# A weighted sum of pairs of rows: from four buffers of 12 tokens to three rooms of 16, combined token by token

## The chip, the cores and the metric

The kernel runs on one core of a Trainium2 chip. The metric is the device time of one execution in microseconds (us); the median of three runs is compared before and after. The profile is one execution recorded by the hardware profiler. Engines that matter here: VectorE (DVE) and ScalarE (ACT) do arithmetic on data in on-chip memory, which has 128 partitions; SyncE (SP) and ACT issue transfers (DMA) between main memory and on-chip memory. Each of the two issuing engines has one transfer queue (q1 for SP, q10 for ACT), and both queues run on the same 16 DMA engines.

## The reference

```python
batch, seq, hidden, n_experts, k = 16, 1024, 512, 8, 2
expert_outputs : float32 [batch, seq, k, hidden]
combine_weights: float32 [batch, seq, k]

def reference(expert_outputs, combine_weights):
    weights = combine_weights[..., np.newaxis]
    return np.sum(expert_outputs * weights, axis=2).astype(np.float32)
```

There are 16 x 1024 = 16384 tokens. For each, two rows of 512 floats (4 KB together) are read, each is multiplied by its own weight, and their sum (2 KB) is written: 67.1 MB in, 33.6 MB out, and 0.13 MB of weights.

## The kernel before

Every partition handles 128 tokens (`per`). The first 120 of them (`main`) come from one contiguous stretch of main memory per partition, so the rows of neighbouring partitions lie 120 x 4 KB = 480 KB apart in the input and 240 KB apart in the output. The last 8 (`LAST`) come from a second region, the end of the arrays, with 32 KB and 16 KB between partitions. `rows` (lines 34 to 38) builds these two views.

The tokens are cut into ten tiles of 12 and one of 8 (`J`, `LAST`, loop at line 68). A tile `et` is one of four buffers of a pool (line 50), 48 KB per partition. Loads are issued by SP (line 75). The first tile is loaded in two pieces, 2 tokens and 10 tokens, and the 2-token piece is cut into rows of 4 KB (line 78); all other loads move one row per partition: 40 KB, 48 KB, and 32 KB for the last tile. A load into a buffer that was used before waits until the store of that buffer has landed.

There are three ways to combine. Tiles 0 to 8 take two long VectorE instructions each: line 84 multiplies the whole tile by the weights, broadcast along the row, and line 85 adds the two halves and writes the sums packed into the front of the same buffer (`ot`). Their store is issued by ACT (line 86). Tile 9 has its first halves scaled by ACT, one token per instruction (line 92), its second halves by one VectorE instruction (line 107), and the sum by another (line 108). Tile 10, the last, is worked token by token: ACT scales the first half (line 92), and VectorE multiplies the second half by its weight and adds (line 96). The stores of tiles 9 and 10 are issued by SP (line 109).

Ahead of the loop, VectorE zeroes a small tile `zt` (line 56), and ACT issues, in this order: a store of `zt` to 16 spots of the output that are overwritten later (line 58), the load of the weights of the main tokens, 960 B per partition, the load of the weights of the last 8 tokens, 64 B per partition (line 62), and a one-column activation that brings in the activation table (line 66). `tc.issue_after` keeps this order.

Waits between engines are made by the framework from the regions that instructions read and write, and the order of instructions on each engine is the framework's own.

Of the kernel before, what the change touches and what calls it, by code (L numbers as in the profile page):

```python
# [1 line left out]

# [4 lines left out]


@with_exitstack
def kernel(  # L10
    ctx: ExitStack,
    tc: tile.TileContext,
    expert_outputs: bass.AP,
    combine_weights: bass.AP,
    out: bass.AP,
):

    nc = tc.nc  # L20
    b, s, k, h = expert_outputs.shape
    assert k == 2
    n = b * s
    P = nc.NUM_PARTITIONS
    per = n // P
    assert per * P == n
    J, LAST = 12, 8
    main = per - LAST
    assert main % J == 0
    eo = expert_outputs.rearrange("b s k h -> (b s) (k h)")  # L30
    cw = combine_weights.rearrange("b s k -> (b s) k")
    o = out.rearrange("b s h -> (b s) h")

    def rows(x):

        a = x[0 : P * main, :].rearrange("(p t) f -> p t f", p=P)
        b = x[P * main : n, :].rearrange("(p t) f -> p t f", p=P)
        return lambda t, c: a[:, t : t + c, :] if t < main else b[:, t - main : t - main + c, :]

    eo, cw, o = rows(eo), rows(cw), rows(o)  # L40

    dt = mybir.dt.float32
    mult = mybir.AluOpType.mult
    add = mybir.AluOpType.add
    copy = mybir.ActivationFunctionType.Copy

    last = main // J

    wpool = ctx.enter_context(tc.tile_pool(name="w", bufs=1))
    ipool = ctx.enter_context(tc.tile_pool(name="in", bufs=4))  # L50

    wt = wpool.tile([P, per * k], dt)


    zt = wpool.tile([16, 128], dt)
    nc.vector.memset(zt, 0.0)  # L56
    first = out.rearrange("b s h -> (b s) h")[0 : P * main, :].rearrange("(q t) h -> q (t h)", q=16)
    ahead = nc.scalar.dma_start(out=first[:, 0:128], in_=zt)  # L58

    with tc.issue_after(ahead.ins):  # L60
        for t, c in ((0, main), (main, LAST)):
            nc.scalar.dma_start(
                out=wt[:, k * t : k * (t + c)].rearrange("p (t k) -> p t k", k=k), in_=cw(t, c)
            )
        warm = wpool.tile([P, 1], dt)
        nc.scalar.activation(out=warm, in_=nc.const_aps.tensor(1.0, (P, 1), dt), func=copy)  # L66

    for g in range(last + 1):
        et = ipool.tile([P, J, k * h], dt)

        ot = et.rearrange("p j f -> p (j f)")[:, 0 : J * h].rearrange("p (j f) -> p j f", f=h)
        t0, c = g * J, J if g < last else LAST

        for a, m in ((0, 2), (2, c - 2)) if g == 0 else ((0, c),):
            nc.sync.dma_start(  # L75
                out=et[:, a : a + m],
                in_=eo(t0 + a, m),
                max_dma_last_dim=k * h * 4 if g + a == 0 else None,
            )
        if g < last - 1:  # L80

            wb = wt[:, g * J * k : (g + 1) * J * k].unsqueeze(2).to_broadcast([P, J * k, h])
            ek = et.rearrange("p j (k h) -> p (j k) h", k=k)
            nc.vector.tensor_tensor(out=ek, in0=ek, in1=wb, op=mult)  # L84
            nc.vector.tensor_tensor(out=ot, in0=et[:, :, 0:h], in1=et[:, :, h : 2 * h], op=add)  # L85
            nc.scalar.dma_start(out=o(t0, c), in_=ot)
            continue


        for i in range(c):  # L90
            t = t0 + i
            nc.scalar.activation(  # L92
                out=et[:, i, 0:h], in_=et[:, i, 0:h], func=copy, scale=wt[:, 2 * t : 2 * t + 1]
            )
            if g == last:
                nc.vector.scalar_tensor_tensor(  # L96
                    out=ot[:, i, :],
                    in0=et[:, i, h : 2 * h],
                    scalar=wt[:, 2 * t + 1 : 2 * t + 2],
                    in1=et[:, i, 0:h],  # L100
                    op0=mult,
                    op1=add,
                )
        if g < last:
            w1 = wt.rearrange("p (t k) -> p t k", k=k)[:, t0 : t0 + c, 1:2]
            x1 = et[:, :, h : 2 * h]
            nc.vector.tensor_tensor(out=x1, in0=x1, in1=w1.to_broadcast([P, c, h]), op=mult)  # L107
            nc.vector.tensor_tensor(out=ot, in0=et[:, :, 0:h], in1=x1, op=add)  # L108
        nc.sync.dma_start(out=o(t0, c), in_=ot[:, 0:c])


# [1 line left out]
_INS = ['expert_outputs', 'combine_weights']  # L113
_OUTS = [((16, 1024, 512), 'float32')]


# [23 lines left out]
```

## Time and profile before

| quantity | value |
|---|---|
| time, median of 3 runs | 239.11 us (239.08 to 239.12) |
| span of the profiled execution | 237.3 us |
| DVE busy | 194.1 us (82%), 29 instructions |
| ACT busy | 14.0 us (6%), 22 instructions |
| main memory read / written | 67.24 MB / 33.56 MB |
| load of a 12-token tile, issue to landing (median) | 29.9 us |
| store of a 12-token tile from ACT, issue to landing (median) | 33.0 us |
| load of the main weights, issue to landing | 17.0 us |
| last load landed | 219.8 us |
| last store issued / landed | 226.5 us / 236.5 us |

The span is counted from the first instruction to the last of the profiled execution, the time also holds what lies around it. "Busy" is the time in which an engine executed instructions; a transfer's time from issue to landing includes its turns behind other transfers on the same engines.

SP, which issues all loads, mostly waits until a buffer is free again:

```profile
SPq L75 <- DMA out_dram<-et: 174.1, 7, 45.8
SPq L75 <- DMA et<-in_expert_outputs_dram: 15.0, 2, 12.2
SPq L109 <- DVE et L108: 14.1, 1, 14.1
SPq L109 <- DMA et<-in_expert_outputs_dram: 10.3, 2, 7.8
```

The columns are the waiting queue and line, what it waited for, the total in us, how often, and the longest.

### The profile page before, as it was taken

What the parts mean: (1) busy time and instruction counts of PE and PEld (TensorE: products, weight loads), DVE (VectorE), ACT (ScalarE), POOL (GpSimd) and SP (SyncE); (2) the same over time, 40 slices, a digit from 0 to 9 for tenths busy, and PEclk for the clock granted to TensorE, in tenths of its full rate; (3) what the DMA queues carried; (4) which work ended last, traced back from release to release, by engine and by line L of the source; (5) the groups of instructions that cost most, each with busy time, mean ns of one, the idle gap of its engine ahead of it and who ended that gap; (6) DMA issues with size and microseconds to landing.
All of it is one profiled execution on the core that took longest, in us unless ns stands there. A gap on an engine that the chain in (4) does not pass through costs nothing.

```text
span 237.3 us, 157 instructions
## 1 busy us (share of the span) xinstructions
DVE 194.1 (82%) x29; ACT 14.0 (6%) x22; POOL 0.2 (0%) x4
## 2 busy tenths in 40 slices
DVE  0008999999999999999999889969996998785710
ACT  2000000000000000000000000000000000740800
POOL 0000000000000000000000000000000000000000
DMA  7999999989899999999898999999998979999997
GB/s 289 452 474 398 398 448 480 398 356 505 352 443 435 427 464 464 398 398 530 348 514 348 447 418 443 464 464 398 398 522 348 522 344 451 464 398 442 406 434 309
DMA packets 3760, 100.80 MB, mean 425 GB/s; under 512 B 544, under 2 KB 688, under 8 KB 944
## 3 DMA queue, kind: packets, MB, share of 16 engines
q1 hardware_dynamic: 2144, 72.35, 71.0%
q10 hardware_dynamic: 1616, 28.45, 27.9%
HBM read 67.24 MB, written 33.56 MB: 425 GB/s over the span
## 4 chain that ended last, share of the span: by engine, by line
DMA 59%; DVE 34%; ACT 2%; ACTq 0%; DVEq 0%; issue 0%; SPq 0%
DMA out_dram<-et 29%; DMA et<-in_expert_outputs_dram 23%; DVE et L84 22%; DVE et L85 11%; DMA wt<-in_combine_weights_dram 7%; ACT et L92 2%; DVE et L96 1%; DVEq L135 0%; ACTq L135 0%; ACTq L58 0%; DVE zt L56 0%; DVEq L84 0%; SPq L75 0%; ACTq L92 0%
## 5 line engine op out<-in xcount | busy, mean ns | idle before, releaser
L84 DVE TENSOR_TENSOR et<-et,wt 128x12288 f32<-128x12288 f32 x9 | 116.6, 12955 | 24.1 <-DMA wt<-in_combine_weights_dram 17.5
L85 DVE TENSOR_TENSOR et<-et 128x6144 f32<-128x6144 f32 x9 | 59.0, 6557 | 0.3
L92 ACT ACTIVATE et<-et,wt 128x512 f32<-128x512 f32 x20 | 12.5, 708 | 208.6 <-DMA et<-in_expert_outputs_dram 208.6
L96 DVE SCALAR_TENSOR_TENSOR et<-et,wt 128x512 f32<-128x512 f32 x8 | 5.6, 746 | 3.9 <-ACT et L92 3.6
L107 DVE TENSOR_TENSOR et<-et,wt 128x6144 f32<-128x6144 f32 x1 | 6.6, 6557 | 2.3 <-DMA et<-in_expert_outputs_dram 2.3
L108 DVE TENSOR_TENSOR et<-et 128x6144 f32<-128x6144 f32 x1 | 6.6, 6558 | 0.9 <-ACT et L92 0.9
L66 ACT ACT_TABLE_LOAD x1 | 1.3, 1283 | 2.4 <-issue 2.4
L56 DVE MEMSET zt<- 16x128 f32 x1 | 0.2, 165 | 0.8 <-PEq L124 0.8
L66 ACT ACTIVATE warm<-const-float32-1.0 128x1 f32<-128x1 f32 x1 | 0.2, 202 | 0.0
L124 POOL MEMSET const-bfloat16-1.0<- 128x1 bf16 x1 | 0.1, 102 | 0.0
L124 POOL MEMSET const-uint8-127<- 128x1 uint8 x1 | 0.1, 101 | 0.0
L124 POOL MEMSET const-float32-0.0<- 128x1 f32 x1 | 0.1, 99 | 0.2 <-issue 0.2
L124 POOL MEMSET const-float32-1.0<- 128x1 f32 x1 | 0.1, 98 | 0.0
## 6 DMA issues: line engine op xcount, KB each, us to landing
et<-in_expert_outputs_dram SPq DMA_DIRECT2D x9, 6144.0 KB, 29.9
out_dram<-et ACTq DMA_DIRECT2D x9, 3072.0 KB, 33.0
et<-in_expert_outputs_dram SPq DMA_DIRECT2D x1, 5120.0 KB, 17.0
et<-in_expert_outputs_dram SPq DMA_DIRECT2D x1, 4096.0 KB, 25.1
out_dram<-et SPq DMA_DIRECT2D x1, 3072.0 KB, 14.6
out_dram<-et SPq DMA_DIRECT2D x1, 2048.0 KB, 10.0
et<-in_expert_outputs_dram SPq DMA_DIRECT2D x1, 1024.0 KB, 5.0
wt<-in_combine_weights_dram ACTq DMA_DIRECT2D x1, 120.0 KB, 17.0
```

The source lines that it names most:

```text
L56: nc.vector.memset(zt, 0.0)
L66: nc.scalar.activation(out=warm, in_=nc.const_aps.tensor(1.0, (P, 1), dt), func=copy)
L84: nc.vector.tensor_tensor(out=ek, in0=ek, in1=wb, op=mult)
L85: nc.vector.tensor_tensor(out=ot, in0=et[:, :, 0:h], in1=et[:, :, h : 2 * h], op=add)
L92: nc.scalar.activation(out=et[:, i, 0:h], in_=et[:, i, 0:h], func=copy, scale=wt[:, 2 * t : 2 * t + 1])
L96: nc.vector.scalar_tensor_tensor(out=ot[:, i, :], in0=et[:, i, h : 2 * h], scalar=wt[:, 2 * t + 1 : 2 * t + 2], in1=et[:, i, 0:h], op0=mul ...
L107: nc.vector.tensor_tensor(out=x1, in0=x1, in1=w1.to_broadcast([P, c, h]), op=mult)
L108: nc.vector.tensor_tensor(out=ot, in0=et[:, :, 0:h], in1=x1, op=add)
L124: nc = _bacc.Bacc("TRN2", target_bir_lowering=False, num_devices=1)
```

## The change

The four buffers become one tile `et` with three rooms of 16 tokens (64 KB per partition each). The tiles have 4, 12 and then seven times 16 tokens; tile g uses room g mod 3. The main part has 112 tokens per partition (448 KB between neighbouring partitions in the input, 224 KB in the output), the last tile's 16 tokens come from the second region (64 KB and 32 KB). No load is cut into smaller rows by hand any more.

All tiles are combined token by token, by `combine`: ACT scales the first half, VectorE multiplies the second half and adds. The sums are packed at the front of the room. For tile 6 alone the tokens are taken from the last to the first and the sums packed at the back of room 0, and tile 7's sums lie at the front of room 1 behind it, so that the two tiles go out in one store of 32 rows of 2 KB, 64 KB per partition. There are eight stores for nine tiles. ACT issues the first six; SP issues the pair's and the last. After a store is issued, SP's next load into that room follows in program order (`load(g + ROOMS)`).

The weights of the main tokens are loaded by SP, between load 0 and load 1; those of the last 16 tokens by ACT behind the store of `zt`. `tc.manual_schedule()` keeps the instructions of each engine in the order in which the program lists them.

```diff
-    J, LAST = 12, 8
-    main = per - LAST
+    ROOM, ROOMS = 16, 3
+    TILES = [4, 12, 16, 16, 16, 16, 16, 16, 16]
+    STORES = [[0], [1], [2], [3], [4], [5], [6, 7], [8]]
+    main = per - TILES[-1]
+    starts = [sum(TILES[:g]) for g in range(len(TILES))]
...
-    wpool = ctx.enter_context(tc.tile_pool(name="w", bufs=1))
-    ipool = ctx.enter_context(tc.tile_pool(name="in", bufs=4))
-    wt = wpool.tile([P, per * k], dt)
+    pool = ctx.enter_context(tc.tile_pool(name="all", bufs=1))
+    et = pool.tile([P, ROOMS * ROOM, k * h], dt)
+    halves = et.rearrange("p j (k h) -> p (j k) h", k=k)
+    wt = pool.tile([P, per * k], dt)
...
+    def load(g):
+        at, c = g % ROOMS * ROOM, TILES[g]
+        nc.sync.dma_start(out=et[:, at : at + c], in_=eo(starts[g], c))
+
+    def weights(q, t, c):
+        q.dma_start(out=wt[:, k * t : k * (t + c)].rearrange("p (t k) -> p t k", k=k), in_=cw(t, c))
+
+    def combine(g, up):
+        at, c = g % ROOMS * ROOM, TILES[g]
+        base = k * at + (ROOM if up else 0)
+        for i in range(c - 1, -1, -1) if up else range(c):
+            t = k * (starts[g] + i)
+            x0, x1 = halves[:, k * (at + i), :], halves[:, k * (at + i) + 1, :]
+            nc.scalar.activation(out=x0, in_=x0, func=copy, scale=wt[:, t : t + 1])
+            nc.vector.scalar_tensor_tensor(
+                out=halves[:, base + i, :], in0=x1, scalar=wt[:, t + 1 : t + 2], in1=x0, op0=mult, op1=add
+            )
+        return base
...
-        for t, c in ((0, main), (main, LAST)):
-            nc.scalar.dma_start(
-                out=wt[:, k * t : k * (t + c)].rearrange("p (t k) -> p t k", k=k), in_=cw(t, c)
-            )
...
+    with tc.manual_schedule():
+        nc.vector.memset(zt, 0.0)
+        ahead = flat[0 : P * main, :].rearrange("(q t) h -> q (t h)", q=16)
+        nc.scalar.dma_start(out=ahead[:, 0:128], in_=zt)
+        weights(nc.scalar, main, per - main)
         nc.scalar.activation(out=warm, in_=nc.const_aps.tensor(1.0, (P, 1), dt), func=copy)
...
-        for a, m in ((0, 2), (2, c - 2)) if g == 0 else ((0, c),):
-            nc.sync.dma_start(
-                out=et[:, a : a + m],
-                in_=eo(t0 + a, m),
-                max_dma_last_dim=k * h * 4 if g + a == 0 else None,
-            )
-        if g < last - 1:
-            wb = wt[:, g * J * k : (g + 1) * J * k].unsqueeze(2).to_broadcast([P, J * k, h])
-            ek = et.rearrange("p j (k h) -> p (j k) h", k=k)
-            nc.vector.tensor_tensor(out=ek, in0=ek, in1=wb, op=mult)
-            nc.vector.tensor_tensor(out=ot, in0=et[:, :, 0:h], in1=et[:, :, h : 2 * h], op=add)
-            nc.scalar.dma_start(out=o(t0, c), in_=ot)
-            continue
...
+        load(0)
+        weights(nc.sync, 0, main)
+        for g in range(1, ROOMS):
+            load(g)
+        for j, st in enumerate(STORES):
+            bases = [combine(g, up=len(st) == 2 and g == st[0]) for g in st]
+            c = sum(TILES[g] for g in st)
+            q = nc.sync if j >= len(STORES) - 2 else nc.scalar
+            q.dma_start(out=o(starts[st[0]], c), in_=halves[:, bases[0] : bases[0] + c, :])
+            for g in st:
+                if g + ROOMS < len(TILES):
+                    load(g + ROOMS)
```

More of the change, by code (lines that the diff above doesn't have):

```diff
@@ L26 @@
     assert per * P == n
-    J, LAST = 12, 8
-    main = per - LAST
[L29 to L32, printed above, removed]
-    def rows(x):
[L36 to L40, printed above, removed]
+    ROOM, ROOMS = 16, 3
+    TILES = [4, 12, 16, 16, 16, 16, 16, 16, 16]
+    STORES = [[0], [1], [2], [3], [4], [5], [6, 7], [8]]
+    assert sum(TILES) == per and [g for st in STORES for g in st] == list(range(len(TILES)))
+    main = per - TILES[-1]
+    starts = [sum(TILES[:g]) for g in range(len(TILES))]
+    def rows(x):
+        first = x[0 : P * main, :].rearrange("(p t) f -> p t f", p=P)
+        second = x[P * main : n, :].rearrange("(p t) f -> p t f", p=P)
+        return lambda t, c: first[:, t : t + c, :] if t < main else second[:, t - main : t - main + c, :]
+    flat = out.rearrange("b s h -> (b s) h")
+    eo = rows(expert_outputs.rearrange("b s k h -> (b s) (k h)"))
+    cw = rows(combine_weights.rearrange("b s k -> (b s) k"))
+    o = rows(flat)
     dt = mybir.dt.float32
@@ L45 @@
     copy = mybir.ActivationFunctionType.Copy
-    last = main // J
-    wpool = ctx.enter_context(tc.tile_pool(name="w", bufs=1))
-    ipool = ctx.enter_context(tc.tile_pool(name="in", bufs=4))
-    wt = wpool.tile([P, per * k], dt)
[L55 to L60, printed above, removed]
-        for t, c in ((0, main), (main, LAST)):
-            nc.scalar.dma_start(
-                out=wt[:, k * t : k * (t + c)].rearrange("p (t k) -> p t k", k=k), in_=cw(t, c)
-            )
-        warm = wpool.tile([P, 1], dt)
-        nc.scalar.activation(out=warm, in_=nc.const_aps.tensor(1.0, (P, 1), dt), func=copy)
@@ L68 @@
[L68 to L72, printed above, removed]
-        for a, m in ((0, 2), (2, c - 2)) if g == 0 else ((0, c),):
-            nc.sync.dma_start(
-                out=et[:, a : a + m],
-                in_=eo(t0 + a, m),
-                max_dma_last_dim=k * h * 4 if g + a == 0 else None,
-            )
-        if g < last - 1:
-            wb = wt[:, g * J * k : (g + 1) * J * k].unsqueeze(2).to_broadcast([P, J * k, h])
-            ek = et.rearrange("p j (k h) -> p (j k) h", k=k)
-            nc.vector.tensor_tensor(out=ek, in0=ek, in1=wb, op=mult)
-            nc.vector.tensor_tensor(out=ot, in0=et[:, :, 0:h], in1=et[:, :, h : 2 * h], op=add)
-            nc.scalar.dma_start(out=o(t0, c), in_=ot)
-            continue
[L90 to L93, printed above, removed]
-            )
[L95 to L109, printed above, removed]
@@ new lines @@
+    pool = ctx.enter_context(tc.tile_pool(name="all", bufs=1))
+    et = pool.tile([P, ROOMS * ROOM, k * h], dt)
+    halves = et.rearrange("p j (k h) -> p (j k) h", k=k)
+    wt = pool.tile([P, per * k], dt)
+    zt = pool.tile([16, 128], dt)
+    warm = pool.tile([P, 1], dt)
+    def load(g):
[3 more added lines that the diff above has]
+        q.dma_start(out=wt[:, k * t : k * (t + c)].rearrange("p (t k) -> p t k", k=k), in_=cw(t, c))
@@ new lines @@
+    with tc.manual_schedule():
[3 more added lines that the diff above has]
+        weights(nc.scalar, main, per - main)
+        nc.scalar.activation(out=warm, in_=nc.const_aps.tensor(1.0, (P, 1), dt), func=copy)
+        load(0)
[5 more added lines that the diff above has]
+            c = sum(TILES[g] for g in st)
+            assert bases[-1] == bases[0] + sum(TILES[g] for g in st[:-1])
+            q = nc.sync if j >= len(STORES) - 2 else nc.scalar
[3 more added lines that the diff above has]
+                    load(g + ROOMS)
```

## The prediction

> **What bounds the kernel now.** I read the transfer rows first, because the kernel does three arithmetic operations on every pair of floats that it loads.
>
> ```profile
> DMA  7999999989899999999898999999998979999997
> DMA packets 3760, 100.80 MB, mean 425 GB/s; under 512 B 544, under 2 KB 688, under 8 KB 944
> q1 hardware_dynamic: 2144, 72.35, 71.0%
> q10 hardware_dynamic: 1616, 28.45, 27.9%
> ```
>
> The two queues together fill 98.9% of sixteen engines' span. Fine windows show where the rest is:
>
> ```profile
> 2.00:3.00 1.00, 0.00 (x0) 0.62 (x1) 0.00 (x0) 1.00 0.70 172
> 20.00:40.00 20.00, 19.97 (x3) 0.00 (x0) 0.00 (x0) 1.00 1.00 433
> 40.00:60.00 20.00, 19.96 (x3) 0.00 (x0) 0.00 (x0) 1.00 0.98 413
> 235.00:236.00 1.00, 0.00 (x0) 0.00 (x0) 0.00 (x0) 1.00 0.62 262
> 236.00:237.00 1.00, 0.00 (x0) 0.00 (x0) 0.00 (x0) 1.00 0.00 0
> ```
>
> The columns are the window, its length, DVE, ACT and POOL busy time, clock, DMA share and GB/s. Transfers run without a hole from the ramp at the start to a cut-off at 236; a share over 1 in neighbouring windows only means that a packet is counted where it ends. So the end is set by how long the transfer engines need for their bytes. The arithmetic is hidden, though DVE is busy for 194 of 237 us:
>
> ```profile
> L84 DVE TENSOR_TENSOR et<-et,wt 128x12288 f32<-128x12288 f32 x9 | 116.6, 12955 | 24.1 <-DMA wt<-in_combine_weights_dram 17.5
> L85 DVE TENSOR_TENSOR et<-et 128x6144 f32<-128x6144 f32 x9 | 59.0, 6557 | 0.3
> L92 ACT ACTIVATE et<-et,wt 128x512 f32<-128x512 f32 x20 | 12.5, 708 | 208.6 <-DMA et<-in_expert_outputs_dram 208.6
> L96 DVE SCALAR_TENSOR_TENSOR et<-et,wt 128x512 f32<-128x512 f32 x8 | 5.6, 746 | 3.9 <-ACT et L92 3.6
> ```
>
> The chain of waits puts 34% on DVE, but during those stretches the transfers ran at full rate; it tells what released what, not what would save time.
>
> **An account of the 237.3 us.** The packet records give one packet's time on its engine: 4 KB 0.159 us, 16 KB 0.611, 24 KB 0.912, 32 KB 1.213, 48 KB 1.815. Every 8 KB adds 0.301 us, which is 27.2 GB/s an engine, 435.2 for sixteen; 100.80 MB take 231.6 us by that. Starts of neighbouring 4 KB packets on one engine are 0.155 us apart, where 4 KB at 27.2 GB/s are 0.1506, so a packet costs about 0.005 us besides its bytes. There are 3760/16 = 235 packets an engine (26 of them semaphore writes): 1.2 us. In the first three microseconds 0.77 us are lost (first packets of 4 KB took 0.195 to 1.07 us in place of 0.159). When the first real store joins, 16 load packets started near 41 took 1.93 to 2.33 us and 15 near 47 took 1.91 to 2.25, about 0.55 us lost in all. 231.6 + 1.2 + 0.77 + 0.55 = 234.1; the packets run from 1.79 to 236.14, which is 234.35, the last 0.2 being engines that finish apart. Ahead lie 1.79 us, behind 1.2 (landing 0.34, then the closing barrier), together the span of 237.3. The median of the runs, 239.11, is 1.8 above it; I take these 1.8 as fixed.
>
> **Part by part.** DVE loses nine pairs of 12.96 + 6.56 us, two instructions of 6.56 and eight of 0.75; it gains 128 of 0.75. ACT goes from 20 to 128 instructions of 0.71. Both are costed at nothing, with the transfers as cover. What matters is the time of one tile from landing to its last instruction. In the last tile of before, eight DVE instructions took 5.78 us and started 0.76 after ACT's first; their starts were 0.86 apart for the first three, 0.66 after. So 4 tokens take 4.0 us, 12 take 9.3, 16 take 12. If that cover were gone, 12 us would stand open at the end.
>
> *Packets.* Loads: before 16 (the 4 KB pieces) + 8 + 72 + 8 = 104 an engine; after 8 + 8 + 7 x 8 = 72. Stores: before 72 + 8 + 8 = 88, after 8 + 8 + 32 + 8 + 8 = 64. Weights (16) and the zero tile (1) stay. Semaphore packets 26 to 20. In sum 235 to 173: 62 x 0.005 = -0.31 us. The bytes stay. A 64 KB packet is not in the trace; by the line it takes 2.418. If a 64 KB row goes as two packets, 64 more an engine come back (+0.32).
>
> *Start.* The first load has 16 KB rows in place of 4 KB ones. Its cold first packets aren't shown; the loss is bounded by none (-0.77) and by the loss of before on top of itself (+0.77). I take -0.1: idle engines between small packets (13 to 15 busy between 2.1 and 2.8) cost some 0.1 and go, the first-touch latency stays.
>
> *First store.* The dip of 0.55 can stay (0) or go (-0.55). I leave it. Until 41 the kernel only loads, and 48 KB packets took 1.819 to 1.831 there; stores start at about 17 now, and that saves 0.004 a packet or so: -0.05.
>
> *Weights.* The 112 tokens' weights leave ACT's queue, where they took 17.0 us to land because each of 8 packets an engine took turns with a load packet; on SP's they follow load 0 and need 8 x 0.04. SP issues four transfers at the start, as before; load 1 is issued one slot of 0.46 us later, behind load 0's 4.9 us. Nothing. The 16 tail tokens' weights stay on ACT and are wanted at about 207.
>
> *Token-wise waits.* ACT now issues a store behind its tile's DVE work; queued behind it is only the next tile, which waits for its load anyway. Regions of one tile don't wait for each other: the two transfers into `wt` were in flight together, and DVE started on the first at 18.5 while the second landed at 33.0. So one `et` for all rooms is no wait in itself.
>
> *Three rooms.* Load g+3 waits for store g. Does a queue run dry? The queues take turns by packet, so a load and a store of 16 tokens take 8 x (2.418 + 1.213) = 29 us together. Step by step: load 0 drains at 7.2, weights at 7.6, store 0 is issued at 12, load 1 drains at 23, store 0 at 37 (its 8 KB packets wait turns behind load 2's 64 KB ones), load 3 is issued there; load 2 drains at 47, store 1 at 63, load 3 at 74, and from there everything repeats with 29: stores 2, 3, 4, 5 drain at 92, 121, 150, 180, loads 4 to 7 at 103, 132, 161, 187. Each load is issued 9 to 10 us before the one ahead has drained, and each store lies queued 5 us before the one ahead ends. Load 8 is issued at 180 with load 7 still moving until 187. Then it has the engines to itself until 206; tile 7 is combined at 199.5, so the pair's 64 KB rows are queued 7 us in time and last until 225.6; tile 8, landed at 207, is combined at 219, 6 us in time; its store drains at 235.3. No hole, the tightest cover being 5 us.
>
> The sum: -0.31 - 0.1 - 0.05 = -0.46, rounded to -0.5: span 236.8, time **238.6**.
>
> **The pitch.** Rows of the main part lie 448 KB apart (input), 480 before. In before, packets took their straight-line time at 480 KB, and at 32 KB in the tail; the slowest undisturbed read-only packet, 1.831 for 1.815, is 0.9% more. That row is the bound: 0.9% of 154 us of load bytes is +1.4 us; the other end is 0. I take 0, since 48 KB packets beside stores took 1.815 throughout.
>
> The Trainium skill, "DMA: Bandwidth & Descriptors", section "Latency and other measured facts", speaks against the change: it gives 207 GB/s a direction for rows 512 KiB apart against 214 padded, and less for larger powers of two. By 207/214 the estimate would be 8 us more; 448 KB is seven times 64 KB and no power of two; the trace has no row at either of these pitches, and at 480 KB it shows no loss.
>
> **Rivals.** (1) The saving is given back: 64 KB rows cut in two (+0.32), or the longer instruction streams of ACT and DVE (20 to 128, 29 to about 130) fetched while running; six 8 KB fetches lie ahead of the span in the trace, 0.31 to 0.57 us of an engine each. The program does need more code; against it speaks that one engine's delay only shows if it ends last. 238.6 + 0.32 to 0.6 is 238.9 to 239.2. Chance 0.12.
> (2) Slower, by the pitch: load packets over 2.418 from tile 2 on, at +1.4: 240.0. It decides from 0.6% on a load packet. Chance 0.10.
> (3) Slower, by the end: no third store is queued while tiles 6 and 7 wait for one another, so load 8 alone must hide tile 7's arithmetic. It decides once a token takes over 1.14 us ((206 - 187.5)/16). If ACT and DVE alternated (0.71 + 0.75), 16 tokens would take 23.4: a hole of 5 at 206 and one of 4 before the last store: 247.6. The 5.78 us for eight tokens speak against. Chance 0.04.
> (4) The one tile makes hidden waits, so the overlap isn't what the code says: a store's issue to landing of some 25 us laid open once would give 263. Chance 0.02.
>
> **How the numbers follow.** The fed queue holds 0.72, its own range 237.9 (start loss and half of the dip gone) to 239.1 (start worse by 0.5). A measurement of this kernel tells about 0.2%, 0.48 us, from no change: below 238.63 is faster. Of the 0.72 I give 0.42 to faster, 0.30 to the same band; rival 1 adds 0.08 to same and 0.04 to slower through a fetch on the last engine and a worse start; rivals 2 to 4 add 0.16 to slower. The range runs from 237.9 to 239.9: it holds case 1 and reaches toward rival 2's 240.0.
>
> **What would show it.** Right: 2768 packets, 100.80 MB, DMA tenths of 9 throughout, load packets of 2.42, DVE near 95 us, the weights landed by 9 us, load 8 issued before load 7 has landed. 3792 packets mean cut rows. A hole in the windows near 187 or 206 is rival 3; a lower rate with full share is rival 2. The prediction falls if the last packet ends later than 236.1 with 2768 packets.

## The result and the profile after

The changed kernel takes 240.58 us (median of 8 executions, 240.53 to 241.05) against 239.13 for the kernel before on the same chip: 1.006 times as long, with a 95% interval of 1.0048 to 1.0072. That is 1.45 us slower, where 0.5 us less was forecast. The profiled execution took 240.75.

The page of the changed kernel, its transfer rows:

```profile
DMA  7999999999999999989899999989899989899994
DMA packets 2771, 100.83 MB, mean 422 GB/s; under 512 B 448, under 2 KB 592, under 8 KB 592
q1 hardware_dynamic: 1728, 79.81, 77.9%
q10 hardware_dynamic: 1040, 21.00, 20.4%
q14 instruction: 3, 0.02, 0.0%
```

There are 2768 data and semaphore packets, as counted in the prediction, and three more on a third queue that the page of before doesn't have: instructions, fetched while the kernel runs. Transfers have no hole, and the two arithmetic engines are far from being a bound:

```profile
L74 DVE SCALAR_TENSOR_TENSOR et<-et,wt 128x512 f32<-128x512 f32 x128 | 87.2, 745 | 132.1 <-ACT et L73 130.3
L73 ACT ACTIVATE et<-et,wt 128x512 f32<-128x512 f32 x128 | 79.4, 708 | 135.6 <-DMA et<-in_expert_outputs_dram 130.3
```

The schedule is the predicted one. In the timeline, tile 7 starts at 189.1 and the pair's store is issued at 201.0, while load 8 (issued at 181.9) moves until 206.8 to 208.1:

```profile
189.12 9.91 ACT L73 ACTIVATE et<-et,wt 128x512 f32<-128x512 f32 x16 [15.32 <-DMA et<-in_expert_outputs_dram]
189.87 11.07 DVE L74 SCALAR_TENSOR_TENSOR et<-et,wt 128x512 f32<-128x512 f32 x16 [14.16 <-ACT et L73]
200.97 19.70 SPq L96 DMA_DIRECT2D out_dram<-et  x2
```

The time went where the prediction had no term. Fine windows at the end (window, length, the engines' busy time, clock, DMA share, GB/s; a packet is counted in the window in which it starts):

```profile
234.00:235.00 1.00, 0.00 (x0) 0.00 (x0) 0.00 (x0) 1.00 1.06 459
235.00:236.00 1.00, 0.00 (x0) 0.00 (x0) 0.00 (x0) 1.00 0.46 197
236.00:237.00 1.00, 0.00 (x0) 0.00 (x0) 0.00 (x0) 1.00 0.08 33
237.00:238.00 1.00, 0.00 (x0) 0.00 (x0) 0.00 (x0) 1.00 0.00 0
```

In before no packet of data starts after 236; here one still does, a store row of 32 KB that takes 1.21 us, hence the share of 0.08. When each engine wrote its semaphore for the last transfer says the same more sharply (us behind the first engine, from the trace's packet records):

```
before: first at 235.70  0 .02 .11 .14 .18 .21 .21 .24 .25 .25 .26 .27 .32 .34 .41 .43
after:  first at 235.76  0 .01 .09 .15 .17 .20 .21 .23 .23 .33 .55 1.10 1.12 1.29 1.33 1.79
```

The first engine ends where it did. Five engines end 0.7 to 1.4 us later than any did before, and the kernel waits for the last one. Bytes done against 27.2 GB/s an engine give the mean over the engines: 2.89 us behind at 235.5, where before it was 2.51. So of 1.41 us by which the last packet ends later (236.14 to 237.55), 0.38 are in the mean and 1.03 in the spread (the last engine is 1.24 behind the mean, 0.21 before).

**Two things made engines late.** The first is a stall when the first stores join. The packets are timed against the straight line of 0.301 us per 8 KB. In the changed kernel load packets of 48 KB lose 0.03 to 0.31 us at 13 to 22, when store 0 joins, and those of 64 KB lose 0.25 to 1.09 at 35 to 42, when store 1 joins; in the mean 0.32 and 0.79 us an engine. In before it is 0.56, at 41 to 49. The windows show the second one (few packets start from 35 to 40, since those that started near 37 are drawn out):

```profile
30.00:35.00 5.00, 3.85 (x6) 2.13 (x4) 0.00 (x0) 1.00 1.03 441
35.00:40.00 5.00, 0.00 (x0) 0.00 (x0) 0.00 (x0) 1.00 0.74 256
40.00:45.00 5.00, 0.00 (x0) 0.00 (x0) 0.00 (x0) 1.00 1.17 505
```

The stall of before, in its own windows:

```profile
40.00:45.00 5.00, 5.00 (x1) 0.00 (x0) 0.00 (x0) 1.00 0.98 393
45.00:50.00 5.00, 5.00 (x1) 0.00 (x0) 0.00 (x0) 1.00 0.92 378
```

It is uneven: load 2 drains on twelve engines between 47.57 and 47.81, on the other four 2.0 us later, and a tile later these four are still 1.05 to 1.23 behind. The second thing is the fetches. VectorE has 208 instructions on record, ACT 152 (48 and 52 before, with their semaphore waits). Fetches of 8 KB take 0.309 us on one engine at 83.7 (VectorE is then at its 70th instruction), 93.2 (ACT at its 62nd) and 217.4 (VectorE at its 200th). The load packet beside each is lengthened by 0.533, 0.241 and 0.458. With the fetch itself that is 0.84, 0.55 and 0.77 us, and the list of offsets changes by those amounts: from load 3 to load 4 one engine moves from 0.18 to 1.02 and one from 0 to 0.55, and from load 8 to the pair's store one from 1.02 to 1.79. The records don't name a packet's engine; by these offsets both VectorE fetches fell on one and the same engine, the one that ends last.

Two theories follow: F, the fetches set the end, and S, the uneven stall does. P, the 448 KB pitch, is out by the packets: 64 KB take 2.418 us in the median, which is on the line.

### The profile page after: what moved, and what is told of

Read it like the earlier page. It is cut to its first block, busy times and chain, and to the rows that moved or that the text cites. A ratio compares the mean times of both kernels' runs of the same rounds, so it can differ in the third digit from the quotient of the medians.

```text
span 239.0 us, 414 instructions
## 1 busy us (share of the span) xinstructions
DVE 87.4 (37%) x129; ACT 80.9 (34%) x130; POOL 0.2 (0%) x4
## 4 chain that ended last, share of the span: by engine, by line
DMA 80%; DVE 7%; ACT 4%; issue 1%; DVEq 0%; ACTq 0%; SPq 0%
DMA out_dram<-et 39%; DMA et<-in_expert_outputs_dram 38%; DVE et L74 7%; ACT et L73 4%; DMA wt<-in_combine_weights_dram 3%; DVEq L125 0%; ACTq L125 0%; SPq L62 0%; DVEq L74 0%; ACTq L73 0%
## 5 line engine op out<-in xcount | busy, mean ns | idle before, releaser
L74 DVE SCALAR_TENSOR_TENSOR et<-et,wt 128x512 f32<-128x512 f32 x128 | 87.2, 745 | 132.1 <-ACT et L73 130.3
L73 ACT ACTIVATE et<-et,wt 128x512 f32<-128x512 f32 x128 | 79.4, 708 | 135.6 <-DMA et<-in_expert_outputs_dram 130.3
```

The costliest lines, as they stand in the source:

```text
L73: nc.scalar.activation(out=x0, in_=x0, func=copy, scale=wt[:, t : t + 1])
L74: nc.vector.scalar_tensor_tensor(out=halves[:, base + i, :], in0=x1, scalar=wt[:, t + 1 : t + 2], in1=x0, op0=mult, op1=add)
```

## The experiments

**Tiles 4 and 5 by wide instructions.** A form for a whole tile, made of the instructions that the kernel before used for its tile 9:

```diff
+    def combine_wide(g):
+        at, c = g % ROOMS * ROOM, TILES[g]
+        for i in range(c):
+            t = k * (starts[g] + i)
+            x0 = halves[:, k * (at + i), :]
+            nc.scalar.activation(out=x0, in_=x0, func=copy, scale=wt[:, t : t + 1])
+        w1 = wt.rearrange("p (t k) -> p t k", k=k)[:, starts[g] : starts[g] + c, 1:2]
+        x1 = et[:, at : at + c, h : 2 * h]
+        nc.vector.tensor_tensor(out=x1, in0=x1, in1=w1.to_broadcast([P, c, h]), op=mult)
+        nc.vector.tensor_tensor(out=halves[:, k * at : k * at + c, :], in0=et[:, at : at + c, 0:h], in1=x1, op=add)
+        return k * at
...
-            bases = [combine(g, up=len(st) == 2 and g == st[0]) for g in st]
+            bases = [combine_wide(g) if g in (4, 5) else combine(g, up=len(st) == 2 and g == st[0]) for g in st]
```

> The changed kernel, but tiles 4 and 5 take two wide VectorE instructions in place of 16 token-wise ones each (ACT as it was), so VectorE's stream is some 40 instructions shorter. Theory F (fetches of instructions while running delay one transfer engine, and the slowest engine sets the end): the fetch at 217 goes, the one near 84 and ACT's near 93 stay, and the last engine is then one that ends 1.33 us after the first in place of 1.79: 0.46 us less, 240.1. Theory S (the stall when the first stores join, larger and more uneven than before, is all of it): 240.6, unchanged. Theory P (448 KB pitch): 240.6.

Measured: 243.46 us, against all theories. The fetch at 217 is gone, but the wide form keeps a tile 6.8 us longer (18.7 from ACT's first instruction to the store's issue, 11.9 token by token), store 4 is issued at 124.6, 2.3 us after store 3 has drained on the first engine, and everything behind slips: load 8 is issued at 186.4 in place of 181.9, 1.2 us before load 7 drains. Load 8's first packets then lose 0.03 to 1.0 us, and its last ones 0.2 to 2.0 when the pair's store follows. Fine windows of this run:

```profile
204.00:206.00 2.00, 0.00 (x0) 0.00 (x0) 0.00 (x0) 1.00 1.80 524
206.00:208.00 2.00, 0.00 (x0) 0.00 (x0) 0.00 (x0) 1.00 0.13 33
208.00:210.00 2.00, 0.00 (x0) 0.00 (x0) 0.00 (x0) 1.00 1.06 459
```

Between 206 and 208 a single packet starts, since those that started near 205 take 3.3 to 4.4 us in place of 2.4. The run says nothing for or against F, since it changed the order of the queues too.

**Tiles 0 and 1 by wide instructions** (the same function, `g in (0, 1)`):

> The changed kernel, but the small tiles 0 and 1 take two wide VectorE instructions each; tiles 2 to 8 and their latencies stay, so the late loads keep their cover, which was lost with tiles 4 and 5 made wide. VectorE's stream is some 20 instructions shorter and ends short of its second fetch. Theory F (fetches while running): two fetches left (VectorE's near 84, ACT's near 93), the fetch at 217 gone, the last engine 1.3 us behind the first in place of 1.79: 240.1. If the time is set by the stalls or the pitch alone: 240.6.

Measured: 244.01 us. The fetch at 217 is gone (one at 243.5, behind the last instruction of the span, has come), and the slip came in all the same: tile 1's store is issued 4.9 us later (38.8), load 8 at 186.5, and the same two losses appear, 0.58 us an engine at 187 and 1.4 at 205. It is a second miss with the same signs: in both runs load 8 joined 1.0 to 1.2 us before its queue ran dry, and both took 2.9 to 3.4 us more than the changed kernel. Why its packets are drawn out stays open.

**The kernel before with instructions that do nothing.**

```diff
+    tiny = wpool.tile([P, 16], dt)
     for g in range(last + 1):
+        if g < last:
+            for e in range(16):
+                nc.vector.memset(tiny[:, e : e + 1], 0.0)
```

> The kernel before, with 160 one-column VectorE clears that nobody reads, done while VectorE waits for the weights. Transfers, pitch and stores are those of before. Theory F: two instruction fetches appear, on one transfer engine, 0.76 to 0.84 us each with what they delay; that engine lay 0 to 0.43 us behind the first, the last one at 0.43, so the end moves by 1.1 to 1.6: 240.2 to 240.7. Theories S and P: 239.1, unchanged.

Measured: 242.09 us, 3.0 more than before, and more than expected. VectorE runs the 160 clears while it waits for the weights; the transfers are issued as in before. Its page's queues, and then windows of its end:

```profile
q1 hardware_dynamic: 2144, 72.35, 70.2%
q10 hardware_dynamic: 1616, 28.45, 27.6%
q14 instruction: 2, 0.02, 0.0%
```

```profile
235.00:236.00 1.00, 0.00 (x0) 0.00 (x0) 0.00 (x0) 1.00 0.66 279
236.00:237.00 1.00, 0.00 (x0) 0.00 (x0) 0.00 (x0) 1.00 0.04 16
237.00:238.00 1.00, 0.00 (x0) 0.00 (x0) 0.00 (x0) 1.00 0.08 33
238.00:239.00 1.00, 0.00 (x0) 0.00 (x0) 0.00 (x0) 1.00 0.04 16
```

Packets and bytes of q1 and q10 are those of before, two fetches were added, and for the last 2.7 us one engine works alone: fifteen end 0 to 0.38 us behind the first, one 3.13. Its path is in the offsets: 1.18 behind after the first fetch (6.6 us), 2.27 after the stall of the first store, where it lost 1.07 and then 0.58 while the others lost about 0.55, and 3.13 after the second fetch (215.0). So an engine that is late when the stores join loses more there, which the expectation hadn't counted.

**The changed kernel with one more fetch.**

```diff
+    tiny = pool.tile([P, 16], dt)
...
+        for e in range(128):
+            nc.vector.memset(tiny[:, e % 16 : e % 16 + 1], 0.0)
         load(0)
```

> The changed kernel with 128 one-column VectorE clears ahead of tile 0 that nobody reads; transfers are the same. Theory F: one more VectorE fetch, three on the same engine, so the last engine ends 0.77 us later, and up to 1.1 more if the engine that is late already loses more in the stall at 37 to 42, as it did in the kernel before with its clears: 241.4 to 242.5. Without theory F: 240.6, or 0.1 more for the few tenths that tile 0 waits.

Measured: 242.14 us, as F has it. There are four fetches, at 6.5, 86.2, 96.7 and 218.7; the last engine is 2.4 behind the first after load 8 and 3.20 at the end, where it was 1.79. Its page's row, and windows of its end:

```profile
q14 instruction: 4, 0.03, 0.0%
```

```profile
235.00:236.00 1.00, 0.00 (x0) 0.00 (x0) 0.00 (x0) 1.00 0.16 66
236.00:237.00 1.00, 0.00 (x0) 0.00 (x0) 0.00 (x0) 1.00 0.15 66
237.00:238.00 1.00, 0.00 (x0) 0.00 (x0) 0.00 (x0) 1.00 0.08 33
```

**No small tiles, single stores.**

```diff
-    TILES = [4, 12, 16, 16, 16, 16, 16, 16, 16]
-    STORES = [[0], [1], [2], [3], [4], [5], [6, 7], [8]]
+    TILES = [16] * 8
+    STORES = [[g] for g in range(8)]
```

> The changed kernel with eight tiles of 16 and eight single stores: no tiles of 4 and 12, so no small early stores; pitch, packet sizes and instruction count as in the changed kernel. Theory S in the form that the two small early stores make the stall: one stall of about 0.55 us in place of two that sum to 1.2, with the fast engines 0.6 us earlier, but the engine with VectorE's two fetches still 1.6 behind: 240.0. S in the form that 64 KB load packets make it: 1.0 or more lost at the one first store: 240.6. Theory P: 240.6.

Measured: 243.89 us. The part on the stall came out: nothing at 13 to 22, and 0.80 us at 35 to 42, the same on all engines (0.73 to 0.97), so that the load under way (the second tile's) drains within 0.66. But without the pair nothing covers the last tile's arithmetic, and the queues ran dry: tile 7 landed near 218, its store was issued at 230.1, and no packet started between 228 and 230. So the pair has its use, and the next version keeps it.

**No small tiles, with the pair.** Rooms are shifted by one so that the pair's rooms lie side by side:

```diff
-    STORES = [[g] for g in range(8)]
+    STORES = [[0], [1], [2], [3], [4], [5, 6], [7]]
-        at, c = g % ROOMS * ROOM, TILES[g]
+        at, c = (g + 1) % ROOMS * ROOM, TILES[g]
```

> Eight tiles of 16 with the sixth and seventh stored as one 64 KB row, so that the hole of 2.5 us before the last store of the eight single stores is closed. Theory: the 0.4 us that the two small early stores cost on every engine is saved, fast engines end at 235.4, but VectorE's fetches hold one engine 1.6 to 2.2 us behind: 239.9 to 240.6. If the small tiles were the whole cause: 239.1 or less.

Measured: 240.58 us (eight of ten executions 240.3 to 241.0, two near 242.7). The stall takes 0.64 us an engine in place of 1.11, the mean over the engines at 235.5 is 2.42 behind in place of 2.89, the second tile's load drains within 0.48, and the time is the same as the changed kernel's, because VectorE's engine ends 1.73 behind the first and the next one 0.65. Windows of its end:

```profile
234.00:235.00 1.00, 0.00 (x0) 0.00 (x0) 0.00 (x0) 1.00 1.21 524
235.00:236.00 1.00, 0.00 (x0) 0.00 (x0) 0.00 (x0) 1.00 0.01 0
236.00:237.00 1.00, 0.00 (x0) 0.00 (x0) 0.00 (x0) 1.00 0.08 33
```

So taking the uneven stall away alone gains nothing.

**The changed kernel without its last fetch.** Tile 6 waits for tile 7 anyway, so its wide form costs no time; it packs to the back in five adds (tokens 15, 14, 12 to 13, 8 to 11, 0 to 7), each of which writes only where nothing is still to be read. Tile 0 is wide too. VectorE has 188 instructions on record in place of 208.

```diff
+        for a, b in ((15, 16), (14, 15), (12, 14), (8, 12), (0, 8)) if up else ((0, c),):
+            y = et[:, at + a : at + b]
+            nc.vector.tensor_tensor(out=halves[:, base + a : base + b, :], in0=y[:, :, 0:h], in1=y[:, :, h : 2 * h], op=add)
...
+            bases = [(combine_wide if g in (0, 6) else combine)(g, up=len(st) == 2 and g == st[0]) for g in st]
```

> The changed kernel, but tile 0 (4 tokens) and tile 6, which waits for tile 7 anyway and has 14 us to spare, take wide VectorE instructions. VectorE has 20 instructions less and ends just short of its second fetch, and unlike with tiles 0 and 1 or 4 and 5 made wide no large store comes later than in the changed kernel. Theory F with the uneven stall: the fetch at 217 is gone, the end is set by an engine that the stall at 35 to 42 left 1.3 us behind: 240.1 (239.9 to 240.2). If the fetch cost nothing: 240.6. If a late load 8 again meets a drained queue: 242 or more, with load 8 issued after 185.

Measured: 240.47 us (240.01 to 241.15). In the span the third fetch is gone; on its page:

```profile
q14 instruction: 2, 0.02, 0.0%
```

The time falls by 0.1 where 0.5 was forecast, but the span falls by 0.4 (238.8 to 238.4, the median of each kernel's executions). Here, and with tiles 0 and 1 wide, the time is 1.9 to 2.2 us longer than the span; in every other kernel of this document it is 1.7 to 1.8 longer. These two alone have a further fetch of 8 KB behind the span (here at 240.8). So the transfers gained about what was forecast, and some 0.1 to 0.3 us come back behind them; that the late fetch is their cause fits, but no run tests it.

The profiled execution is the slowest of the five. There the stall left two engines 1.42 and 1.47 behind; ACT's fetch at 95.7 then fell on the second of them, which ends last, 2.05 behind. How far behind the stall leaves its worst engine varies between the profiled executions with small tiles, from 0.65 us (tiles 4 and 5 wide) to 1.9 (tiles 0 and 1 wide).

**Both at once.** No small tiles, the pair, and tiles 1 to 4 in the wide form (in the version with the pair alone these stores are issued 8 to 9 us before the store ahead has drained; 1.8 to 2.2 us of that are left, and no load slips): 122 VectorE instructions on record in place of 207.

```diff
+            bases = [(combine_wide if g in (1, 2, 3, 4) else combine)(g, up=len(st) == 2 and g == st[0]) for g in st]
```

> Eight tiles of 16 with the sixth and seventh stored together, and tiles 1 to 4 by wide VectorE instructions: 124 VectorE instructions in place of 210, one VectorE fetch (near 170) and one ACT fetch. Stores there have 8 us of cover and the wide form takes 5.6 longer, so the queues keep their order. Theory F with the even stall of one large first store: fast engines end at 235.5, the last one 0.5 to 0.9 behind: 239.1 to 239.7. If the small tiles and the fetches together were not the cause of the loss: 240.6.

Measured: median 239.61 us; seven of twelve executions lie between 239.45 and 239.65, one of them the profiled one. The other five are between 241.3 and 243.1; no profile shows one of these, nor one of the two slow ones of the version with the pair alone, and what happens in them stays open. In the profile the fetches are down to two, and the last engine ends 0.96 behind the first. Its page's row, and windows of its end:

```profile
q14 instruction: 2, 0.02, 0.0%
```

```profile
234.00:235.00 1.00, 0.00 (x0) 0.00 (x0) 0.00 (x0) 1.00 1.21 524
235.00:236.00 1.00, 0.00 (x0) 0.00 (x0) 0.00 (x0) 1.00 0.08 33
236.00:237.00 1.00, 0.00 (x0) 0.00 (x0) 0.00 (x0) 1.00 0.00 0
```

The transfers differ from the version with the pair alone in nothing but when some stores are issued; some 85 VectorE instructions fewer, and with them one fetch, are worth 1.0 us in the medians (240.58 to 239.61) and 0.8 in the profiled spans (238.6 to 237.8). What is left over the kernel before, 0.5 us, fits the spread that the two remaining fetches leave, 0.96 in place of 0.43.

**Is the stall a first touch?** In both kernels the zero tile was stored to one spot per partition (128 rows) in place of 16 spots.

```diff
-    zt = pool.tile([16, 128], dt)
+    zt = pool.tile([P, 128], dt)
-        ahead = flat[0 : P * main, :].rearrange("(q t) h -> q (t h)", q=16)
+        ahead = flat[0 : P * main, :].rearrange("(q t) h -> q (t h)", q=P)
```

> The changed kernel, but the zero tile that is stored ahead has 128 rows of 512 B, one at the start of every partition's stretch of the output, in place of 16. If the stall at the first stores is a first touch of each output stretch: it goes from the windows 13 to 22 and 35 to 42, 0.8 to 1.2 us less on every engine, and the engines end closer, so that the engine with the fetches is last: 239.5 to 239.9. If it is not: 240.6, or 0.1 more for the 112 extra packets.

> The kernel before, with the zero tile stored to 128 rows, one per partition's stretch of the output, in place of 16. If the stall at its first real store (0.55 us at 41 to 49) is a first touch of each stretch: 0.3 to 0.55 us less, 238.6 to 238.8. If it comes from the first large store itself, as the stall at 35 to 42 did in the changed kernel: 239.1.

Measured: 240.83 and 239.27 us. The large stall stays: 0.91 us an engine at 34 to 42 in the changed kernel, 0.56 in the kernel before. So it is not a first touch of each partition's stretch of the output. The small loss at 13 to 22 falls from 0.32 to 0.09 an engine, but that does not show that the touch did it: with the zero tile in 16 spots the same loss is 0.07 with tiles 4 and 5 wide, which is the same program up to there, and 0.09 to 0.24 in the other three versions with small tiles. It varies from execution to execution. What causes the large one isn't settled: it comes once in each of these kernels, with the first store of 24 KB packets or more, whether that begins at 35 or at 41. In the changed kernel and in before no later store has it; in the two versions whose load 8 came late, the pair's store has 1.3 to 1.4 us an engine beside it.

## Why the prediction was wrong

Its steps on the schedule held. Packets fell from 3760 to 2768; no hole opened; load 8 was issued before load 7 had landed; the weights landed at 8.7; a 64 KB row is one packet of 2.418 us; 448 KB between rows costs nothing on the steady packets, so rival 2 did not come, and the rule on large pitches, which the prediction weighed and set aside, did not bear on this case. VectorE was busy for 87 us where 95 were forecast, with no effect. Regions of the one tile made no false waits. Its own sign of being wrong came: 2768 packets, and the last one ends at 237.55, after 236.1.

Its sum failed in three places; the first is the step that decided.

First, the account ended with "the last 0.2 being engines that finish apart" and carried that over as a constant. The spread is what changed most: the last engine is 1.24 us behind the mean in place of 0.21, +1.03. This kernel ends with its slowest engine, and the sum had been made for their mean.

Second, the fetches, which make the last of that spread. The prediction had them as rival 1, at "0.31 to 0.57 us of an engine each", taken from the fetches ahead of the span, and covered them with "one engine's delay only shows if it ends last". A fetch costs 0.55 to 0.84 us, because the 64 KB packet beside it is drawn out as well; two of the three hit the same engine, and 0.84 + 0.77 is nearly four times the 0.43 by which engines lay apart. The engine hit twice does end last. That three would come could not be read from the trace of before, which has none in its span at 48 and 52 instructions.

Third, the first store: "The dip of 0.55 can stay (0) or go (-0.55). I leave it." No upper bound was set. It became 1.11: 0.32 beside the small early store, which the versions without small tiles don't have, and 0.79 in the main stall, which left four engines 1.05 to 1.23 behind. With the small tiles gone the main one is 0.64 to 0.80, level (the engines 0.37 to 0.66 apart after it). With them it is 0.62 to 0.97, and 0.65 to 1.9. So the small tiles go with the unevenness, though one profiled execution with them was as level as one without; the cause of the stall itself stays open.

In the mean the terms add up: -0.31 for 62 packets, nothing for the start (0.82 us lost, 0.81 in before, where -0.1 was taken), +0.55 for the stalls (1.11 for 0.56), and +0.14 for three fetches over sixteen engines are +0.38, measured 0.38. With the spread of 1.03 the last packet comes 1.4 later. That is in the profiled execution, whose time is 1.6 above before; the median is 1.45 above.

Neither cause alone is the answer. Without the small tiles the time was 240.58, because VectorE's engine still ended 1.73 behind; without the last fetch it was 240.47, with 0.4 less in the span; with both changes it was 239.61, in the median of executions that vary more than before. None of the versions tried beats the kernel before. Its long VectorE instructions, at 82% busy, look like waste beside the transfers and are what keeps the instruction stream short.

Three slips of the prediction bear on none of this. A window counts a packet where it starts, not where it ends; (206 - 187.5)/16 is 1.16, not 1.14; and the low end of its range comes to 237.7 by its own terms, not 237.9.

The Trainium skill, "Runtime: NRT & Kernel Launch", section "Instruction fetch mechanics", has fetches in blocks of 16 KiB, 256 instructions, with a crossing "mostly hidden". These runs show packets of 8 KB, with VectorE at its 70th and 200th instruction on record in the changed kernel (at its 163rd and 191st in the kernel before with clears), and a crossing that VectorE's instructions don't show (tile 3's take 11.07 us with a fetch beside them, as other tiles' do) but the transfer engine that carries it does; with all sixteen full, the measurement decides.

## What to carry to other kernels

In a kernel whose transfer engines are full from start to end, keep an account of the slowest of the sixteen, not only of their sum: look at when each writes its semaphore for the last transfer. There instructions are traffic too: here about every 130 on VectorE's record brought a fetch that held one engine for 0.55 to 0.90 us. One long instruction in place of sixteen short ones saves such fetches, as long as it doesn't delay a store or a load. Before a stage is made longer, check how long ahead the next load is queued; in the two versions that lost 4.4 of 5.5 us of that lead, the time grew by some 3 us.

## What the runs showed of the hardware

Eight KB of instructions cost one transfer engine 0.55 to 0.84 us beside 64 KB packets (0.84 to 0.90 beside 32 and 40 KB in the kernel before with clears), and two of them left it 3.1 us behind when a stall fell between. The first store of 24 KB packets or more draws out the load packets beside it by 0.56 to 0.97 us an engine. A packet costs about 5 ns besides its bytes from 4 KB to 64 KB. When load 8 joined 1.0 to 1.2 us before its queue ran dry, its last packets, 17 us later, were held for 0.2 to 2.0 us in both versions where that happened, and in none where the last load joined 3.3 us ahead or more; the cause stays open.
